# Hybrid encoder layer on one core: the wide output group's block sums formed by accumulating DRAM transfers, and one sum kept in DRAM

## The chip, the cores and the metric

One core of one Trainium2 chip. The metric is device time in microseconds (us); the median of three runs is given, with the lowest and highest. A profile shows one execution, with the time from its first to its last instruction (the span).

## What is computed

The layer is `x + mixed @ w_out`. x is 512 tokens by 2048, all float32. `mixed` has 2048 columns: 1024 from attention (8 heads, 2 key/value heads, QK norm, axial rope) and 1024 from a bidirectional gated linear recurrence (LRU), each normalised and gated by a SiLU of its own projection.

```
h = rms_norm(x, norm_w)
q, k, v, g_attn, xr, g_lru = split(h @ w_in)
attn_out = attention_group(q, k, v, ...)
lru_out = lru_group(xr, ...)
mixed = concat(rms_norm(attn_out) * silu(g_attn), rms_norm(lru_out) * silu(g_lru))
out = x + mixed @ w_out
```

The change touches only how parts of `w_out` are brought to the last half of the output columns.

## The kernel before

Every float32 operand is split into a high part (ScalarE's copy with rounding, "hi") and a low part (VectorE's subtraction, "lo"), and a product is three matmuls: hi by hi, hi by lo, lo by hi (`mm3`, L147 to L150; in the output, `product`, L845). Weights come as 256 rows by 512 columns (512 KB) through a ring of three buffers: `wraw` (L192, transfer L198, on SyncE's queue) and `wsplit` (L203: hi on ScalarE L209, lo on VectorE L210). The order on TensorE is written out by hand. On the other engines a scheduler orders the work by priority: `tc.high_priority(n)` moves work forward, `tc.issue_after(ins)` queues work behind an instruction on that engine. Each engine and each queue runs its list in order.

The stages: the LRU's input (two groups of 512 columns), K and V (`kv_proj`, L1008, woven with the second half of the LRU), Q in two groups (`both`, L1026, woven with K's norm, rope and transposes), attention woven with the gates' projections, then the output. In K and Q GpSimd raises mean squares to the power -1/2 (`rsqrt_mean`, L261 and L262): K's and Q's norms on VectorE (L518) wait for it.

The output has four groups of 512 columns. Groups 0 and 1 are made by `outputs` one after the other; groups 2 and 3 together by `outputs_wide` (L817), "the wide group". There the matrix is cut into 2 by 2 blocks and multiplied with Winograd's seven products (P1, P2, Q3 to Q7). `w_out` is walked in eight pairs of 128-row blocks, in the order 4 to 7, 0 to 3. Of a pair, row block k and column group j give four blocks of 128 by 512: call them B(k, j). The sums that the products need are

- T1 = B(0,0) + B(0,1)
- T2 = B(1,0) + T1
- T3 = B(0,0) + B(1,0)
- T4 = the sum of all four

Pass 1 (L856) takes P1, Q6 and Q5 over the eight pairs: 18 matmuls for each pair. It loads B(0,0) and B(0,1) in one transfer and B(1,0) in another (`raw_blocks`, L832), forms T1 in place of B(0,0) (VectorE, L861) and T2 in place of B(1,0) (L862), and `parts` splits all three (ScalarE L841, VectorE L842). Pass 2 (L909) takes Q3 and P2 of the plain blocks B(1,0) and B(1,1) (`plain`, L894), and Q7 and Q4 of T3 and T4 (`summed`, L899): 24 matmuls for each pair. It loads all four blocks again in two transfers of 512 KB, forms T3 and B(0,1) + B(1,1) in one add of 1024 elements (L903), T4 in a second add (L904), and splits plain and summed blocks apart. So a pair in pass 2 has a plain split and a summed split.

Three raw buffers of [4, 512] are used in turn, two in `aring` and one in `wring`; a buffer is free when its last split is done. The split parts have three buffers in turn too (`wkept`, L722). Between the passes, four adds (L871, L873) and copies (L869, L874) empty PSUM into the result tiles xs[0] ("xt") and xs[1] ("cb"). The residual x is added to them in pass 2 by `residual` (L876): four transfers of 512 KB (L880) into tiles "t4", of which there are two (`bufs=2`), each followed by one add on VectorE (L884): xt, cb, xt, cb. At the end the last products are added and the result leaves (L927, L930).

The TensorE rows of the trace carry the line of the matmul (L148 to L150, L752, L765, L851); "pj" and "mm" are the two kinds of PSUM tiles.

Of the kernel before, what the change touches and what calls it, by code (L numbers as in the profile page):

```python
# [10 lines left out]
F32 = mybir.dt.float32  # L11
F32R = mybir.dt.float32r
AF = mybir.ActivationFunctionType
ALU = mybir.AluOpType
AX = mybir.AxisListType

P = 128
SEQ = 512
DM = 2048
# [39 lines left out]
def hybrid_kernel(  # L59
# [20 lines left out]
    nc = tc.nc  # L80
# [30 lines left out]
    def nm(s):  # L111
        cnt[0] += 1
        return f"{s}_{cnt[0]}"
# [7 lines left out]
    def k2(dt=F32, shape=(P, SEQ)):  # L121
        pool, n, _ = work()
        return pools[pool].tile(list(shape), dt, tag="k2", bufs=n, name=nm("k2"))
# [11 lines left out]
    def pj():  # L135
        return ps.tile([P, SEQ], F32, tag="pj", name=nm("pj"))
# [7 lines left out]
    def f(ap):  # L144
        return ap.bitcast(F32)
# [43 lines left out]
        return vec[:, r : r + 1]  # L189


    def wraw(w, r0, c0, nk=1, queue=nc.sync):  # L192

        raw = wring.tile([P, 2, SEQ], F32, name=nm("wr"))
        src = w[r0 : r0 + 2 * P, c0 : c0 + SEQ].rearrange("(k p) e -> p k e", p=P)
        for k in range(nk):
            ks = slice(k * 2 // nk, (k + 1) * 2 // nk)
            queue.dma_start(raw[:, ks, :], src[:, ks, :])  # L198
            yield raw

    turn_of = [0]
# [131 lines left out]
    def weave(fill, chain):  # L333

        for n in chain:
            for _ in range(n):
                next(fill, None)
# [46 lines left out]
    def lru_half(half, acc):  # L384

        grs = []
        for n in range(4 * half, 4 * half + 4):
            gr = k2(shape=(P, 4, P))
            with tc.high_priority(AHEAD):
                nc.sync.dma_start(gr[:, 0:2, :], lru_wa[:, n].rearrange("d c e -> c d e"))  # L390
                nc.sync.dma_start(gr[:, 2:4, :], lru_wx[:, n].rearrange("d c e -> c d e"))
            grs.append(gr)
        xrs = evac_bc(acc)
        for b in range(0, 4, 2):
            bs = slice(b, b + 2)
            steps = ((6, 4, 8, 4), (10, 5, 8, 5))[half][bs]
            yield from lru_pair(4 * half + b, xrs[bs], grs[bs], steps, 99 if half and b else 0)
# [410 lines left out]
    def part(i, a):  # L808
# [5 lines left out]
            return [t[:, a + 1] for t in mixed[i][1]]  # L814
        return [t[a - 3] for t in sums_of[i]]

    def outputs_wide(c, built):  # L817


        xs = [  # L820
            pools["out"].tile([P, NT, SEQ], F32, tag=t, bufs=1, name=nm(t)) for t in ("xt", "cb")
        ]
        cs = [slice((c + j) * SEQ, (c + j + 1) * SEQ) for j in range(2)]
        rings = [aring, aring, wring]

        def raw_blocks(i, n, turn):

            raw = rings[turn % 3].tile([P, 4, SEQ], F32, name=nm("wr"))
            r0 = mixed[i][0]
            for k in range(2):  # L830
                w = slice(cs[0].start, cs[0].start + min(2, n - 2 * k) * SEQ)
                nc.sync.dma_start(  # L832
                    raw[:, 2 * k : min(n, 2 * k + 2)].rearrange("p j e -> p (j e)"),
                    w_out[r0 + k * P : r0 + (k + 1) * P, w],
                )
            return raw

        def parts(blocks, n):
            hi, lo = (t.rearrange("p n e -> p (n e)") for t in wkept(7))
            hi, lo = (t[:, : n * SEQ].rearrange("p (n e) -> p n e", e=SEQ) for t in (hi, lo))  # L840
            nc.scalar.copy(hi, blocks)  # L841
            nc.vector.tensor_sub(lo, blocks, f(hi))  # L842
            return hi, lo

        def product(k, dst, i, b, n):  # L845
            ah, al = part(i, k[0])
            bh, bl = (t[:, n] for t in b)
            for s in range(2):
                ts_ = slice(s * P, (s + 1) * P)
                for j, (lh, rh) in enumerate(((ah, bh), (ah, bl), (al, bh))):  # L850
                    nc.tensor.matmul(  # L851
                        dst[s], lh[:, ts_], rh, start=i == 0 and j == 0, stop=i == 7 and j == 2
                    )

        p1, q6, q5 = [pj(), pj()], [pj(), pj()], [mm(), mm()]
        for i in range(8):  # L856

            with tc.high_priority(SOON), tc.issue_after(built):
                raw = raw_blocks(i, 3, i)

                nc.vector.tensor_add(raw[:, 0], raw[:, 0], raw[:, 1])  # L861
                nc.vector.tensor_add(raw[:, 2], raw[:, 2], raw[:, 0])  # L862
                b = parts(raw[:, 0:3], 3)
            for k, dst, n in ((P1, p1, 1), (Q6, q6, 2), (Q5, q5, 0)):
                product(k, dst, i, b, n)
        with tc.high_priority(SOON):

            for s in range(2):
                nc.scalar.copy(xs[1][:, 2 + s], p1[s])  # L869
            for s in range(2):  # L870
                nc.vector.tensor_sub(xs[1][:, s], xs[1][:, 2 + s], q6[s])  # L871
            for s in range(2):
                nc.vector.tensor_sub(xs[0][:, 2 + s], q5[s], xs[1][:, s])  # L873
                nc.scalar.copy(xs[0][:, s], xs[0][:, 2 + s])  # L874

        def residual(m, j):  # L876

            with tc.high_priority(SOON):
                xr = pools["fin"].tile([P, 2, SEQ], F32, tag="t4", bufs=2, name=nm("t4"))
                nc.sync.dma_start(  # L880
                    xr, xf[2 * m * P : 2 * (m + 1) * P, cs[j]].rearrange("(t p) e -> p t e", p=P)
                )
            to = xs[j][:, 2 * m : 2 * m + 2]
            nc.vector.tensor_add(to, to, xr)  # L884

        q3, p2, q7, q4 = [mm(), mm()], [pj(), pj()], [pj(), pj()], [mm(), mm()]
        raws = {}

        def given(i):
            if i not in raws:  # L890
                raws[i] = raw_blocks(i, 4, 8 + i)
            return raws[i]

        def plain(i):  # L894
            with tc.high_priority(SOON):
                b = parts(given(i)[:, 2:4], 2)
            return lambda: product(Q3, q3, i, b, 0), lambda: product(P2, p2, i, b, 1)

        def summed(i):  # L899
            with tc.high_priority(SOON):  # L900
                raw = given(i)

                nc.vector.tensor_add(raw[:, 0:2], raw[:, 0:2], raw[:, 2:4])  # L903
                nc.vector.tensor_add(raw[:, 1], raw[:, 1], raw[:, 0])  # L904
                b = parts(raw[:, 0:2], 2)
            product(Q7, q7, i, b, 0)
            product(Q4, q4, i, b, 1)

        for i in range(6):  # L909
            for step in plain(i):  # L910
                step()
            summed(i)
            if 1 <= i < 5:
                residual((i - 1) // 2, (i - 1) % 2)

        summed(6)
        summed(7)
        for steps in zip(plain(6), plain(7)):
            for step in steps:
                step()  # L920

        with tc.high_priority(SOON):

            def add(t, j, acc, op=ALU.add, leave=True, cut=1):
                for m in range(cut):
                    e = slice(m * SEQ // cut, (m + 1) * SEQ // cut)
                    nc.vector.tensor_tensor(xs[j][:, t, e], xs[j][:, t, e], acc[:, e], op=op)  # L927
                    if leave:
                        to = slice(cs[j].start + e.start, cs[j].start + e.stop)
                        nc.sync.dma_start(of[tokens[t], to], xs[j][:, t, e])  # L930

            for s in range(2):
                add(s, 0, q7[s])
                add(s, 1, q7[s], ALU.subtract, False)
            for s in range(2):
                add(s, 1, q4[s])
            for s in range(2):
                add(2 + s, 0, q3[s])
            for s in range(2):
                add(2 + s, 1, p2[s], cut=1 + s)  # L940
# [5 lines left out]
    a1, a2, a3, a4, a5 = [], [], [], [], []  # L946
# [15 lines left out]
    with tc.high_priority():  # L962
        xs, ws = xload(0, 2), wraw(w_in, 0, C_XR, 2, nc.scalar)
        nc.scalar.dma_start(nw_st, norm_w.rearrange("(k p) -> k p", p=P))
        xc, raw = next(xs), next(ws)
# [9 lines left out]
    for step in proj_feat(C_XR, a1, first, given):  # L975
# [8 lines left out]
        c, e = step  # L984
# [17 lines left out]
    fill = proj_feat(C_XR + SEQ, a2)  # L1002
# [5 lines left out]
    def kv_proj():  # L1008
        yield from proj_tok(C_K, a3)
        kvs.extend(  # L1010
            evac_tok(
                a3, lambda: pools["rope"].tile([P, SEQ], F32, tag="kv", bufs=NT, name=nm("kv"))
            )
        )

    weave(kv_proj(), lru_half(1, a2))
    closed("lru")
    opened("rot", "left")
    opened("qkv", "right")
# [6 lines left out]
    def both():  # L1026
        yield from q_proj(C_Q, a4)
        yield from q_proj(C_Q + SEQ, a5)

    fill = both()  # L1030
    weave(fill, kv(kvs))
    drain(fill)

# [22 lines left out]
    fill = gates()  # L1056
# [11 lines left out]
    mixed = [[(NH + 2 * q) * P, None] for q in range(4)] + [[2 * q * P, None] for q in range(4)]  # L1068
# [30 lines left out]
    fill = proj_feat(C_GA + SEQ, acc)  # L1099
# [89 lines left out]
```

## Time and profile before

| what | value |
|---|---|
| median of 3 runs | 661.93 us (661.31 to 662.49) |
| the profiled execution | 660.99 us |
| its span | 659.2 us, mean granted TensorE clock 1.000 |
| TensorE, VectorE, ScalarE, GpSimd busy | 652.4, 500.8, 337.4, 58.9 us |
| moved by DMA | 77.32 MB, 117 GB/s in the mean |
| wide group on TensorE | 577.48 to 653.5 us |

PE is TensorE's matmuls, PEld its weight loads, DVE VectorE, ACT ScalarE, POOL GpSimd, SP SyncE; an engine's name with a q is its queue, or its sequencer. A row of the timeline gives start and duration in us, engine and line, what is written and read, partitions by elements, and in brackets how long the engine was idle before and what ended that. A row of a stage gives its limits, its length, the busy time of PE, PEld, DVE, ACT and POOL (with the number of instructions), the granted clock, the DMA engines' share and GB/s. A row of the chain gives start, duration, and the instructions merged in it. A row of waits gives who waited for whom, the total in us, how often, and the longest. A row of DMA issues ends in KB each and the median us from issue to landing.

### The profile page before, as it was taken

The numbers are of one execution on the slowest core, as the hardware profiler recorded it, in microseconds if no ns is written. First come the engines' busy times: TensorE is split into PE (matmuls) and PEld (weight loads), VectorE is DVE, ScalarE is ACT, GpSimd is POOL, SyncE is SP. The second block draws the span as 40 slices with busy tenths as digits, with TensorE's granted clock in tenths as the row PEclk, the third lists the DMA queues.
The fourth block names the chain that finished last, engine by engine and source line by source line (L and its number), as shares of the span: only waits on it lengthen the run. The fifth ranks groups of instructions, "written<-read, shape, count | busy, mean of one in ns | idle before, by whom it ended". The sixth has DMA issues, their size and how long they took to land.

```text
span 659.2 us, 8994 instructions
## 1 busy us (share of the span) xinstructions
PE 652.4 (99%) x3323; PEld 553.2 (84%) x3323; DVE 500.8 (76%) x822; ACT 337.4 (51%) x582; POOL 58.9 (9%) x79
## 2 busy tenths in 40 slices
PE   8999999999999999999999999999999999999996
PEld 6888888888888888888888888888889999888875
DVE  5889788978688854656955677439989998777995
ACT  3534898589766416444743455335437433233431
POOL 0000000000023303011222212110000000000000
PEclk9999999999999999999999999999999999999999
DMA  8852252323234312322112211232336356375643
GB/s 290 287 142 84 69 164 66 94 64 96 72 121 129 108 53 64 96 65 64 38 60 64 65 45 53 64 96 76 103 110 211 127 178 224 110 230 201 243 140 127
DMA packets 43963, 77.32 MB, mean 117 GB/s; under 512 B 2968, under 2 KB 13328, under 8 KB 43920
## 3 DMA queue, kind: packets, MB, share of 16 engines
q1 hardware_dynamic: 43600, 76.22, 37.5%
q10 hardware_dynamic: 320, 0.53, 0.3%
q8 instruction: 26, 0.43, 0.3%
q14 instruction: 17, 0.14, 0.1%
HBM read 72.54 MB, written 4.19 MB: 116 GB/s over the span
## 4 chain that ended last, share of the span: by engine, by line
PE 98%; DMA 1%; DVE 0%; ACTq 0%; DVEq 0%; issue 0%
PE pj L148 20%; PE pj L150 20%; PE pj L149 20%; PE pj L851 7%; PE pj L752 5%; PE mm L851 5%; PE mm L752 4%; PE mm L148 3%; PE mm L150 3%; PE mm L149 3%; PE mm L765 3%; PE mm L595 2%; PE mm L235 1%; PE pj L301 1%; PE mm L538 1%; DMA wr<-in_w_in_dram 1%
## 5 line engine op out<-in xcount | busy, mean ns | idle before, releaser
L148 PE MATMUL pj<-x,wh 128*128 128x512 f32 x376 | 149.1, 396 | 0.0
L150 PE MATMUL pj<-x,wl 128*128 128x512 f32 x376 | 147.0, 391 | 0.0
L149 PE MATMUL pj<-x,wh 128*128 128x512 f32 x376 | 146.5, 390 | 0.0
L210 DVE TENSOR_TENSOR wl<-wr,wh 128x512 fp32r<-128x512 f32 x144 | 100.8, 722 | 30.0 <-ACT wh L209 29.9
L209 ACT CAST wh<-wr 128x512 fp32r<-128x512 f32 x143 | 85.8, 618 | 73.4 <-PE pj L150 25.7
L150 PEld LDWEIGHTS pj<-x,wl 128*128 128x128 f32 x376 | 70.6, 188 | 15.3
L149 PEld LDWEIGHTS pj<-x,wh 128*128 128x128 f32 x376 | 70.7, 188 | 13.6 <-DVE x L238 0.2
L148 PEld LDWEIGHTS pj<-x,wh 128*128 128x128 f32 x376 | 70.6, 188 | 13.3
L148 PE MATMUL pj<-wh,x 128*128 128x512 f32 x192 | 74.9, 390 | 0.0
L150 PE MATMUL pj<-wh,x 128*128 128x512 f32 x192 | 74.7, 389 | 0.0
L149 PE MATMUL pj<-wl,x 128*128 128x512 f32 x192 | 74.7, 389 | 0.0
L841 ACT CAST wh<-wr 128x1024 fp32r<-128x1024 f32 (+1 forms) x24 | 28.7, 1198 | 52.0 <-PE mm L851 28.6
L597 ACT CAST b<-mm 128x512 fp32r<-128x512 f32 x32 | 18.8, 586 | 61.5 <-PE mm L595 61.5
L583 DVE TENSOR_REDUCE mx<-mm 128x1 f32<-128x512 f32 x32 | 22.0, 689 | 32.9 <-PE mm L150 32.3
L150 PEld LDWEIGHTS pj<-wh,x 128*128 128x128 f32 x192 | 36.0, 188 | 7.6
L148 PEld LDWEIGHTS pj<-wh,x 128*128 128x128 f32 x192 | 36.0, 188 | 7.5
L149 PEld LDWEIGHTS pj<-wl,x 128*128 128x128 f32 x192 | 36.0, 188 | 7.4
L588 POOL TENSOR_SCALAR k<-k,sm 128x512 f32<-128x512 f32 x32 | 24.2, 756 | 123.9 <-DVE sm L587 112.4
L842 DVE TENSOR_TENSOR wl<-wr,wh 128x1024 fp32r<-128x1024 f32 (+1 forms) x24 | 33.5, 1395 | 1.5 <-ACT wh L841 1.3
L598 DVE TENSOR_TENSOR b<-mm,b 128x512 fp32r<-128x512 f32 x32 | 22.1, 689 | 12.1 <-ACT b L597 12.1
L752 PE MATMUL pj<-wh,ml 128*128 128x256 f32 x96 | 27.2, 283 | 0.0
L752 PE MATMUL pj<-wl,mh 128*128 128x256 f32 x96 | 27.2, 283 | 0.0
(249 smaller groups left out, 1350.7 us busy)
## 6 DMA issues: line engine op xcount, KB each, us to landing
wr<-in_w_in_dram SPq DMA_DIRECT2D x71, 512.0 KB, 3.7
wr<-in_w_out_dram SPq DMA_DIRECT2D x40, 512.0 KB, 3.9
b<-in_x_dram SPq DMA_DIRECT2D x7, 512.0 KB, 8.9
out_dram<-xt SPq DMA_DIRECT2D x12, 256.0 KB, 3.2
xt<-in_x_dram SPq DMA_DIRECT2D x8, 256.0 KB, 5.0
wr<-in_w_out_dram SPq DMA_DIRECT2D x8, 256.0 KB, 4.3
t<-in_x_dram SPq DMA_DIRECT2D x4, 512.0 KB, 4.4
k<-in_lru_wa_dram SPq DMA_DIRECT2D x8, 128.0 KB, 3.6
```

Of the source, the lines that this page charges most:

```text
L148: nc.tensor.matmul(acc, lh, rh, start=start, stop=False)
L149: nc.tensor.matmul(acc, lh, rl, start=False, stop=False)
L150: nc.tensor.matmul(acc, ll, rh, start=False, stop=stop)
L209: copy(hi, raw[:, k, :])
L210: nc.vector.tensor_sub(lo, raw[:, k, :], f(hi))
L583: nc.vector.tensor_reduce(mx, sc, axis=AX.X, op=ALU.max, negate=True)
L588: nc.gpsimd.tensor_scalar(p, p, sm, 0.0, op0=ALU.mult, op1=ALU.add)
L598: nc.vector.tensor_sub(ptl[:, :, tt], p3, f(pth[:, :, tt]))
L752: nc.tensor.matmul(dst, lh[:, a, ts_], rh[:, b_, :], start=bank in fresh, stop=last and s == 1 and rh is bh and lh is al, skip_group_check ...
L841: nc.scalar.copy(hi, blocks)
L842: nc.vector.tensor_sub(lo, blocks, f(hi))
L851: nc.tensor.matmul(dst[s], lh[:, ts_], rh, start=i == 0 and j == 0, stop=i == 7 and j == 2)
```

## The change

T1 and T3 are formed in DRAM, long before they are used. During K and the first Q projection, after every two weight loads, SyncE copies B(0,0) of one pair into two DRAM tensors t1 and t3, queued behind the weight load issued last; then GpSimd issues two transfers which add B(0,1) to the one and B(1,0) to the other while moving (`accum_op`). Each waits for its copy. That makes 16 copies and 16 accumulating transfers of 256 KB.

In pass 1 T1 is loaded from t1, and the blocks B(0,1) and B(1,0) in transfers of their own; the add that formed T1 (L861) is gone. T2, formed as before, is also stored to a DRAM tensor t2. In pass 2 T3 and T2 are loaded from DRAM beside B(1,0) and B(1,1), four transfers of 256 KB in place of two of 512 KB; T4 is T2 + B(1,1), one add of 512 elements, and the add of 1024 (L903) is gone. The bytes that are loaded stay the same; eight stores of 256 KB come in.

```diff
+    loads_done = {}
     def wraw(w, r0, c0, nk=1, queue=nc.sync):
...
-            queue.dma_start(raw[:, ks, :], src[:, ks, :])
+            loads_done[queue] = queue.dma_start(raw[:, ks, :], src[:, ks, :]).ins
...
+    t1, t3, t2 = (
+        ctx.enter_context(tc.tile_pool(name=t, bufs=1, space=bass.MemoryType.DRAM)).tile(
+            [DM // (2 * P), P, SEQ + 16], F32, name=nm(t)
+        )[:, :, :SEQ]
+        for t in ("t1", "t3", "t2")
+    )
+    def sums_of_blocks(c):
+        pairs = w_out.rearrange("(m k p) e -> m k p e", k=2, p=P)
+        b12, b11 = (pairs[:, 0, :, (c + j) * SEQ : (c + j + 1) * SEQ] for j in range(2))
+        b22 = pairs[:, 1, :, c * SEQ : (c + 1) * SEQ]
+        for m in range(DM // (2 * P)):
+            with tc.issue_after(loads_done[nc.sync]):
+                for to in (t1, t3):
+                    nc.sync.dma_start(to[m], b12[m])
+            for to, other in ((t1, b11), (t3, b22)):
+                nc.gpsimd.dma_start(to[m], other[m], accum_op=ALU.add)
+            yield
...
-                raw = raw_blocks(i, 3, i)
-                nc.vector.tensor_add(raw[:, 0], raw[:, 0], raw[:, 1])
+                raw, m = raw_tile(i), mixed[i][0] // (2 * P)
+                for n, src in enumerate((t1[m], block(i, 0, 1), block(i, 1, 0))):
+                    nc.sync.dma_start(raw[:, n], src)
                 nc.vector.tensor_add(raw[:, 2], raw[:, 2], raw[:, 0])
                 b = parts(raw[:, 0:3], 3)
+                nc.sync.dma_start(t2[m], raw[:, 2])
...
-                raws[i] = raw_blocks(i, 4, 8 + i)
+                raw, m = raw_tile(8 + i), mixed[i][0] // (2 * P)
+                for n, src in enumerate((t3[m], t2[m], block(i, 1, 0), block(i, 1, 1))):
+                    nc.sync.dma_start(raw[:, n], src)
+                raws[i] = raw
...
-                nc.vector.tensor_add(raw[:, 0:2], raw[:, 0:2], raw[:, 2:4])
-                nc.vector.tensor_add(raw[:, 1], raw[:, 1], raw[:, 0])
+                nc.vector.tensor_add(raw[:, 1], raw[:, 1], raw[:, 3])
                 b = parts(raw[:, 0:2], 2)
...
+    wsums = sums_of_blocks(2)
+    def with_sums(fill, n):
+        for k, _ in enumerate(fill):
+            if k % n == n - 1:
+                next(wsums, None)
+            yield
-    weave(kv_proj(), lru_half(1, a2))
+    weave(with_sums(kv_proj(), 8), lru_half(1, a2))
...
-    fill = both()
+    fill = with_sums(both(), 8)
```

`block(i, k, j)` is B(k, j) of pair i in `w_out`, `raw_tile(turn)` one of the three raw buffers. A projection makes 32 steps over eight loads, so every eighth step is every second load: four pairs in K, four in the first Q.

More of the change, by code (lines that the diff above doesn't have):

```diff
@@ L824, in outputs_wide, with raw_tile, block @@
         rings = [aring, aring, wring]
[L826 to L836, printed above, removed]
+        def raw_tile(turn):
+            return rings[turn % 3].tile([P, 4, SEQ], F32, name=nm("wr"))
+        def block(i, k, j):
+            r0 = mixed[i][0] + k * P
+            return w_out[r0 : r0 + P, cs[j]]
         def parts(blocks, n):
```

## The prediction, made before the result was known

> **What bounds the kernel now.** I read the page first: its span, its first part and its chain.
>
> ```profile
> span 659.2 us, 8994 instructions
> PE 652.4 (99%) x3323; PEld 553.2 (84%) x3323; DVE 500.8 (76%) x822; ACT 337.4 (51%) x582; POOL 58.9 (9%) x79
> PE 98%; DMA 1%; DVE 0%; ACTq 0%; DVEq 0%; issue 0%
> ```
>
> TensorE is both the busy engine and the chain. A busy share can hide small waits, so next come busy time by stage, the chain in order of time in the stage that the change rewrites, and who waited there.
>
> ```profile
> 577.00:654.00 77.00, 77.00 (x339) 62.97 (x337) 62.22 (x66) 27.87 (x26) 0.00 (x0) 1.00 0.58 191
> ```
> ```profile
> 606.04 2.77 PE pj L851 x12
> 608.81 2.72 PE mm L851 x12
> ...
> 619.69 2.72 PE mm L851 x12
> 622.41 2.72 PE pj L851 x12
> 625.13 2.95 PE mm L851 x12
> 628.08 2.90 PE pj L851 x12
> ...
> 653.53 1.10 DVE cb L927 x2
> ```
> ```profile
> PEld mm L851 <- DVE wl L842: 0.4, 1, 0.4
> ```
>
> In the wide group TensorE is busy for 77.00 of 77 us at clock 1.00, and twelve products take 2.72 us, 0.227 each, wherever one looks. Two pieces are longer, 2.95 and 2.90: there alone TensorE waited for VectorE's split (the weight load of the first shows it, wl L842), (2.95 - 2.72) + (2.90 - 2.72) = 0.41 us. That is all that a lighter VectorE can give back here. VectorE's 62.22 busy us are off the path, and the 5.7 us from 653.53 to the end of the span are not touched. So the question is whether anything the change adds makes TensorE wait.
>
> **What it removes.** The built program of the changed kernel has TensorE's and ScalarE's instructions in the same order as before; VectorE loses 16 of 32 adds, SyncE gains 48 transfers, GpSimd 16.
>
> ```profile
> L903 DVE TENSOR_TENSOR wr<-wr x8: 1215/1222/1226, 599.3 to 638.9; 128x1024 f32<-128x1024 f32 x8
> L904 DVE TENSOR_TENSOR wr<-wr x8: 681/683/693, 600.5 to 640.2; 128x512 f32<-128x512 f32 x8
> L861 DVE TENSOR_TENSOR wr<-wr x5: 681/683/691, 576.9 to 594.1; 128x512 f32<-128x512 f32 x5
> ```
>
> Pass 1 loses eight adds of 0.68 (L861), pass 2 eight of 1.22 (L903); the other add of each pass stays. That is 8 x 0.68 + 8 x 1.22 = 15.2 us of VectorE, on the path only for the 0.41 above.
>
> **What moves.** VectorE's order changes in pass 2, and this is where I find the price. The residual's transfers (L880) use two buffers in turn: the third (x for xt's second half) can start only when the add of the first (L884) is done. Before, the third and fourth adds stand well behind:
>
> ```profile
> 602.91 0.80 SPq L832 DMA_DIRECT2D wr<-in_w_out_dram  x2
> ```
> ```profile
> 608.11 1.23 DVE L903 TENSOR_TENSOR wr<-wr 128x1024 f32<-128x1024 f32 x1 [2.35 <-DMA wr<-in_w_out_dram]
> 609.25 1.22 DVE L842 TENSOR_TENSOR wl<-wr,wh 128x1024 fp32r<-128x1024 f32 x1
> 610.38 1.28 DVE L871 TENSOR_TENSOR cb<-cb,pj 128x512 f32<-128x512 f32 x2
> 610.49 0.80 SPq L832 DMA_DIRECT2D wr<-in_w_out_dram  x2
> 611.58 1.28 DVE L873 TENSOR_TENSOR xt<-mm,cb 128x512 f32<-128x512 f32 x2
> ...
> 614.51 1.22 DVE L884 TENSOR_TENSOR xt<-xt,t 128x1024 f32<-128x1024 f32 x1
> 615.76 0.38 SPq L880 DMA_DIRECT2D t<-in_x_dram  x1
> ...
> 621.93 1.22 DVE L884 TENSOR_TENSOR xt<-xt,t 128x1024 f32<-128x1024 f32 x1
> ...
> 625.38 1.22 DVE L842 TENSOR_TENSOR wl<-wr,wh 128x1024 fp32r<-128x1024 f32 x1
> ```
> ```profile
> SPq L880 <- DVE xt L884: 4.4, 1, 4.4
> t<-in_x_dram SPq DMA_DIRECT2D x4, 512.0 KB, 4.4
> ```
>
> The first residual add starts at 614.51, its buffer's next transfer is issued at 615.76 (SyncE waited 4.4 us for exactly this), and the add that uses it stands at 621.93, seven VectorE instructions later. In the changed program's VectorE order the stretch reads: T4 add of pair 2, summed split of pair 0, the four adds of L871/L873, the second residual add (cb), plain split of pair 1, **T4 add of pair 3, first residual add (xt), summed split of pair 1, third residual add (xt), plain split of pair 2**. One split stands between the add that frees the buffer and the add that waits for its refill; behind that wait is a split which TensorE needs.
>
> Step by step, with start-to-start times from the fence: 1.14 us for 1024 elements (609.25 - 608.11), 0.60 for 512 (two from 610.38 to 611.58), 5.2 us from the first issue of a pair's 1 MB to the add (602.91 to 608.11).
> - Pair 2's four transfers start when pass 1's last split has freed their buffer, as before (602.9); I take 603.0. T4 add of pair 2 at 608.2, split of pair 0 at 608.8, free at 609.95.
> - Four adds from 609.95, 4 x 0.60: 612.35; second residual add to 613.5; plain split of pair 1 to 614.65.
> - Pair 3's transfers start at 610.05 into the buffer of pair 0 (before 610.49) and land 5.2 later: T4 add of pair 3 at 615.25 (before, the add stood later, at 616.78, and did not wait). First residual add 615.85 to 617.0, summed split of pair 1 to 618.15.
> - The third residual transfer starts at 617.1 (0.1 after the add, as 615.76 after 614.51 + 1.14) and lands 4.4 later, 621.5. Its add runs to 622.65, the plain split of pair 2 is done at 623.85.
> - TensorE: the piece at 619.69 ends with the first product of pair 2, from 621.05; its second matmul, at 621.28, reads the split's low part. Before, the split of pair 3 ended at 625.38 + 1.22 = 626.60 and the matmul it held came at 625.13 + 7 x 0.227 + 0.23 = 626.95, 0.35 behind. So here: 623.85 + 0.35 = 624.2, **2.9 us late**.
>
> Behind this everything has 2.9 us more: the fourth residual add to 624.95, summed split of pair 2 to 626.1, needed at 624.0 + 2.9 = 626.9; the later pairs are spaced as before. The 0.41 of the two long pieces disappears in the new wait.
>
> Sum: 2.9 - 0.4 = +2.5 us. Its own profiled execution took 660.99 us (1.8 outside the span), so 663.5; the median of three is 0.94 above that: **664.4**.
>
> **What else is added, at nothing.** Copies and accumulations during K and Q: 32 of 256 KB, four per two weight loads.
>
> ```profile
> 185.69 0.37 SPq L198 DMA_DIRECT2D wr<-in_w_in_dram  x1
> ```
> ```profile
> 192.46 0.27 POOL L261 TENSOR_SCALAR rr<-rr 128x2 f32<-128x2 f32 x1 [1.78 <-ACT sh L513]
> 193.87 0.42 DVE L518 TENSOR_TENSOR kv<-kv,rr 128x256 f32<-128x256 f32 x1 [0.19 <-POOL rr L262]
> 197.03 1.88 DVE L210 TENSOR_TENSOR wl<-wr,wh 128x512 fp32r<-128x512 f32 x3
> 211.60 0.68 ACT L501 ACTIVATE ev<-pj,rstd 128x512 f32<-128x512 f32 x1
> ```
> ```profile
> xt<-in_x_dram SPq DMA_DIRECT2D x8, 256.0 KB, 5.0
> ```
>
> SyncE issues the copies behind a weight load, 0.4 us each, in time it otherwise waits. GpSimd's queue is in order: the last two accumulations stand ahead of K's second rsqrt (192.46) and wait for copies issued behind the load of 185.69. No copy between two DRAM tensors is in the trace; by a 256 KB load they land at 186.5 + 5.0 = 191.5. GpSimd's own time to issue one is not in the trace either; the nearest are SyncE's 0.37 and its own 0.27, so 0.3 to 1.5 each, and rsqrt is 0 to 2 us late. VectorE waits with it at 193.87, and the split behind, at 197.03, is late by as much. It feeds Q0's last load: the last bank was evacuated at 211.60, one load is 24 x 0.227 = 5.4 us of products, so it is read from about 206. Some 8 us of cover: cost nothing.
>
> The Trainium skill, "DMA: Bandwidth & Descriptors", section "Specifications", gives about 1 us to the first byte of a DMA issued by GpSimd against 0.6 from SyncE; by an estimate from it rsqrt would be 2 us late, inside the same cover, and the sum stays; no run here shows it yet.
>
> T2's stores: pair 0's T2 is stored in pass 1 and loaded a pass later, eight pairs on (8 x 18 x 0.227 = 33 us), so the two landings do not meet. The eight stores (256 KB) stand between pass 1's loads in SyncE's queue, each behind a VectorE add. The tightest of pass 1's splits, for pair 3, and the piece that reads it:
>
> ```profile
> 585.18 1.75 DVE L842 TENSOR_TENSOR wl<-wr,wh 128x1536 fp32r<-128x1536 f32 x1
> 589.72 2.72 PE pj L851 x12
> ```
>
> It ends at 586.9, 2.8 us early. In the new order it stands ahead of pair 4's add, for which it waited, and comes sooner; stepped in the same way, the later ones end within 1 us of before. So nothing; with the cover gone, up to 3 us.
>
> The same page of the Trainium skill, section "Rules for kernel authors", says that a DMA which reads what an earlier one wrote must wait for its completion, so T2 pays two landings; were store and load close, pass 2's first loads would be late by one more landing, which no run here shows yet.
>
> **The rivals.**
> - *A, the refill is in time, not slower.* If a pair's four transfers land faster than the two before (VectorE is lighter, the DMA engines are 0.58 busy), the whole row of waits moves forward. For no loss the plain split of pair 2 must end by 621.28 - 0.35 = 620.9, the third residual add start by 618.6, its transfer by 614.2, so that pair 3 has landed by 612.3, 2.9 us sooner than I step. Against it: 5.2 us to land, and buffers that TensorE's pace frees. With 1 MB in 4 us the first residual add ends near 615.7 (pass 1's last products hold the adds of L871/L873) and +1.2 is left. At best the 0.41 is won: 661.5.
> - *B, pass 1 goes late too.* SyncE holds the next loads behind each store; if a store's add slips, splits lose their 3 us of cover and TensorE waits there as well, on top: 2.5 + 1 to 3 us, 665.5 to 667.5. For it: six more waits in SyncE's order; against: the step above.
> - *C, GpSimd's wait in K and Q.* If an accumulation holds GpSimd until rsqrt is over 8 us late (copies landing after some 13 us instead of 5), TensorE waits for the rest; at 12 us 4 more, 668. Transfers of this size never took that long here.
>
> **How the numbers follow.** Forecast, one stalled split at +1.4 to +4.5 us: 0.60. A: 0.27. B: 0.10. C: 0.03. The bounds of the forecast's own unknowns (landing of 1 MB 5.0 to 6 us, of 512 KB 3.7 to 5.5) give 663.3 to 666.4. The range reaches into A's best, 661.4, and over B, 667.8. 0.2% is 1.3 us, about what a measurement of this kernel can tell from no change. Slower by more: forecast, B, C, a little of A: 0.73. Within: 0.25. Faster: 0.02.
>
> **What would show it.** Right: in pass 2 a VectorE wait of about 3 us of the third residual add (xt) for `t<-in_x_dram`, a TensorE or weight-load wait of about 3 us for the split next to it near 621, none before 618, and the rest of the chain shifted alike. GpSimd's 16 issues inside 94 to 194 us without a wait of TensorE. Wrong: no gap near 621 (A), gaps from 585 to 606 (B), gaps from 195 to 215 (C).

## The result and the profile after

The changed kernel takes **668.81 us** (median of 4 runs, 667.24 to 669.12) against 661.94 (661.31 to 662.49) for the kernel before: 1.0097 times as long, 95% interval 1.0084 to 1.0110. It is slower, as forecast, but by 6.9 us where 2.5 was forecast, and lies above the range, which ended at 667.8. The profiled execution took 668.51 us.

The page of the changed kernel (span; busy time of each engine; the chain by engine):

```profile
span 666.7 us, 9091 instructions
...
PE 656.2 (98%) x3323; PEld 554.9 (83%) x3323; DVE 488.1 (73%) x806; ACT 337.5 (51%) x582; POOL 73.0 (11%) x95
...
PE 57%; DMA 5%; DVE 3%; SPq 2%; issue 1%; ACT 1%; DVEq 0%; ACTq 0%
```

VectorE is lighter by 12.7 us (500.8 to 488.1), as intended, and nothing came of it. The chain, before TensorE from end to end, now runs through DMA, VectorE and SyncE's queue. The busy time of the wide group and TensorE's waits tell where:

```profile
577.00:654.00 77.00, 72.99 (x311) 58.74 (x310) 45.04 (x45) 27.32 (x26) 0.00 (x0) 0.98 0.64 198
```
```profile
PE pj L871 <- DVE wl L862: 3.1, 2, 2.2
...
PE mm L871 <- DVE wl L862: 0.9, 1, 0.9
PE pj L148 <- ACT ev L504: 0.2, 1, 0.2
```

TensorE idles 4 of 77 us and its clock falls from 1.00 to 0.98. Three waits are for a split (L862), one for ScalarE's emptying of a PSUM bank in Q (L504). The longest, in the timeline of TensorE (start, duration, the idle time in brackets):

```profile
606.81 0.39 PE L871 MATMUL mm<-wh,ev 128*128 128x512 f32 x1
607.04 0.39 PE L871 MATMUL pj<-wh,mh 128*128 128x512 f32 x1
609.63 0.73 PE L871 MATMUL pj<-wl,mh 128*128 128x512 f32 x1 [2.20 <-DVE wl L862]
610.15 0.63 PE L871 MATMUL pj<-wh,ml 128*128 128x512 f32 x1
610.58 0.63 PE L871 MATMUL pj<-wh,mh 128*128 128x512 f32 x1
...
612.71 0.60 PE L871 MATMUL pj<-wh,ml 128*128 128x512 f32 x1
613.14 0.40 PE L871 MATMUL pj<-wh,mh 128*128 128x512 f32 x1
613.38 0.40 PE L871 MATMUL pj<-wl,mh 128*128 128x512 f32 x1
```

Starts that stood 0.23 apart are 2.59 apart at 607.04, and then 0.43 apart from 610.15 to 613.14: seven steps of 0.427 instead of 0.227. One wait is paid twice: 2.36 us at the wait, 0.29 in the first step after it, and 1.4 in the seven slow steps. The granted clock in these slow steps (a row of a stage, for TensorE alone) is 0.50:

```profile
609.75:613.10 3.35, 3.35 (x8) 0.50 0.71 207
```

The two other waits, at 620.86 and 624.83, cost 1.2 each and leave the clock alone. From the start of its first matmul to the start of its last the wide group takes 83.0 us (578.24 to 661.24) where it took 76.5 (577.31 to 653.79): that is +6.5 of the span's +7.5. The rest, 0.93, lies before it: 0.56 at the wait in Q and 0.37 in the first 46 us, where TensorE waits for the first loads and every execution differs (its first real product began at 6.13 before, at 5.89 to 6.97 in the runs below). Hence the table below has a column for the wide group alone.

What the late split stood behind is in VectorE's order:

```profile
587.27 0.69 DVE L883 TENSOR_TENSOR wr<-wr 128x512 f32<-128x512 f32 x1 [1.43 <-DMA wr<-in_w_out_dram]
589.43 0.69 DVE L883 TENSOR_TENSOR wr<-wr 128x512 f32<-128x512 f32 x1 [1.46 <-DMA wr<-in_w_out_dram]
...
596.55 0.69 DVE L883 TENSOR_TENSOR wr<-wr 128x512 f32<-128x512 f32 x1 [4.76 <-DMA wr<-in_w_out_dram]
...
607.21 0.69 DVE L928 TENSOR_TENSOR wr<-wr 128x512 f32<-128x512 f32 x1 [6.03 <-DMA wr<-in_w_out_dram]
607.82 1.75 DVE L862 TENSOR_TENSOR wl<-wr,wh 128x1536 fp32r<-128x1536 f32 x1
...
615.49 0.69 DVE L928 TENSOR_TENSOR wr<-wr 128x512 f32<-128x512 f32 x1 [3.66 <-DMA wr<-in_w_out_dram]
```

The split of pass 1's last pair (607.82, three blocks) stands behind pass 2's first T4 add (L928), and that waited 6.03 us for a transfer. Three adds ahead of it in pass 1 waited too, the last of them 4.76 us. SyncE's queue shows why the one at 596.55 did:

```profile
585.87 0.33 SPq L881 DMA_DIRECT2D wr<-t  x1
587.99 2.48 SPq L885 DMA_DIRECT2D t<-wr  x2
590.51 1.36 SPq L881 DMA_DIRECT2D wr<-in_w_out_dram  x2
```

T1 of pair 6 is requested at 585.87; then SyncE holds at two stores of T2 (L885) until the adds of 587.27 and 589.43 are done, and the pair's two other blocks go out from 590.51, 4.6 us after the first.

### The profile page after: what moved, and what is told of

The parts are those of the page before. It is cut to its first block, busy times and chain, and to the rows that moved or that the text cites. A ratio compares the mean times of both kernels' runs of the same rounds, so it can differ in the third digit from the quotient of the medians.

```text
span 666.7 us, 9091 instructions
## 1 busy us (share of the span) xinstructions
PE 656.2 (98%) x3323; PEld 554.9 (83%) x3323; DVE 488.1 (73%) x806; ACT 337.5 (51%) x582; POOL 73.0 (11%) x95
## 2 busy tenths in 40 slices
DMA packets 53180, 87.81 MB, mean 132 GB/s; under 512 B 3992, under 2 KB 14352, under 8 KB 53136
## 4 chain that ended last, share of the span: by engine, by line
PE 57%; DMA 5%; DVE 3%; SPq 2%; issue 1%; ACT 1%; DVEq 0%; ACTq 0%
PE pj L148 11%; PE pj L150 11%; PE pj L149 11%; DMA wr<-in_w_out_dram 5%; PE pj L755 4%; PE mm L755 3%; PE mm L871 3%; PE pj L871 3%; PE mm L148 2%; PE mm L150 2%; PE mm L149 2%; PE mm L598 2%; PE mm L768 2%; DVE wl L862 1%; SPq L881 1%
## 5 line engine op out<-in xcount | busy, mean ns | idle before, releaser
L150 PEld LDWEIGHTS pj<-x,wl 128*128 128x128 f32 x376 | 70.6, 188 | 15.2
L861 ACT CAST wh<-wr 128x1024 fp32r<-128x1024 f32 (+1 forms) x24 | 28.5, 1196 | 54.6 <-PE mm L871 15.1
L862 DVE TENSOR_TENSOR wl<-wr,wh 128x1024 fp32r<-128x1024 f32 (+1 forms) x24 | 33.4, 1398 | 6.3 <-ACT wh L861 6.3
L838 POOL DMA_DIRECT2D t<-in_w_out_dram x16 | 13.3, 834 | 132.0 <-DMA t<-in_w_out_dram 132.0
L871 PE MATMUL pj<-wl,mh 128*128 128x512 f32 x60 | 24.5, 408 | 3.1 <-DVE wl L862 3.1
```

The lines of the kernel that those rows point to most:

```text
L150: nc.tensor.matmul(acc, ll, rh, start=False, stop=stop)
L871: nc.tensor.matmul(dst[s], lh[:, ts_], rh, start=i == 0 and j == 0, stop=i == 7 and j == 2)
```

## The experiments

After this reading there were two theories for the wide group. **L**: the loads themselves are slower, since a pair comes in four transfers of one block (256 KB) where two double blocks came. **S**: SyncE is held at T2's stores and issues the next loads late. K and Q are a third, smaller item. The results, all beside runs of the kernel before on the same chip (medians 661.2 to 661.9); the last column is worked out as above from each profile, so from one execution:

| run | median us | ratio, 95% interval | wide group on TensorE, us |
|---|---|---|---|
| before | 661.9 | | 76.5 |
| changed kernel | 668.8 | 1.0097 (1.0084 to 1.0110) | 83.0 |
| e1, T2 not stored | 666.4 | 1.0067 (1.0052 to 1.0082) | 81.3 |
| e2, T2 stored by GpSimd | 665.4 | 1.0056 (1.0043 to 1.0069) | 81.5 |
| e3, before + sums in K and Q | 662.7 | 1.0018 (1.0009 to 1.0026) | 78.2 |
| e4, before, single blocks | 666.8 | 1.0078 (1.0066 to 1.0090) | 80.8 |
| e5, before, small extra transfers | 661.8 | 1.0003 (0.9993 to 1.0013) | 76.1 |
| e6, before, 2 KB rows | 664.5 | 1.0044 (1.0029 to 1.0060) | 77.8 |
| e7, changed, long rows in pass 2 | 662.9 | 1.0017 (1.0005 to 1.0029) | 78.0 |
| e8, e7 with all sums in K | 662.7 | 1.0011 (1.0001 to 1.0022) | 78.2 |
| e9, e8 with long rows in pass 1 too | 661.3 | 1.0001 (0.9992 to 1.0011) | 76.0 |
| e10, before, half transfers | 671.3 | 1.0146 (1.0131 to 1.0162) | 87.4 |
| e11, e9 with stores by SyncE | 661.5 | 1.0004 (0.9995 to 1.0013) | 76.1 |

### e1 and e2: T2's stores

e1 leaves out the store and forms T2 again in pass 2, from B(0,1) in place of t2 and a second add:

```diff
-                nc.sync.dma_start(t2[m], raw[:, 2])
...
-                for n, src in enumerate((t3[m], t2[m], block(i, 1, 0), block(i, 1, 1))):
+                for n, src in enumerate((t3[m], block(i, 0, 1), block(i, 1, 0), block(i, 1, 1))):
...
+                nc.vector.tensor_add(raw[:, 1], raw[:, 1], raw[:, 0])
```

e2 only moves it to GpSimd's queue: `nc.gpsimd.dma_start(t2[m], raw[:, 2])`.

> The changed kernel, without T2 in DRAM: no store in pass 1, and in pass 2 B(0,1) is loaded in T2's place and T4 = T3 + B(0,1) + B(1,1), one more add of 512 on VectorE for each pair. The bytes loaded and the number of loads stay. Theory S (the T2 stores stand in SyncE's queue ahead of the next pair's loads, each behind a VectorE add that waits for a load, so loads cannot run ahead): the waits of TensorE in the wide group go, and with them most of the 6.9 us; 661.5 to 663.5 us, what is left being the K and Q part. Theory L (single-block transfers of 256 KB land later than the double blocks before, whatever the queue): waits of TensorE stay, 665 us or more. Theory V (VectorE's order, the next pair's add ahead of the split, is enough alone): 665 or more too, with the wait at the split of pass 1's last pair.

> The changed kernel with T2's eight stores issued from GpSimd's queue, which is empty in this stage; bytes and loads as changed. Theory S: SyncE's loads are free again, no wait of TensorE at the split of pass 1's last pair, 661.5 to 664. If the traffic of the stores (2.1 MB more in the wide group) delays the loads: about as the changed kernel, 667 to 669. Theory L: 665 or more.

Both stay far above before: 2.4 and 3.4 us less than the changed kernel, 4.8 and 3.8 us more than the kernel before beside them. The long stall moves into pass 2's start (behind the matmuls of 613.15 and 613.87, 2.1 us idle each), where TensorE waits for PSUM that VectorE empties late, and both again run some 3 us at spacing 0.427 behind it. The first matmul after it, in e1:

```profile
615.64 0.65 PE L871 MATMUL pj<-wh,mh 128*128 128x512 f32 x1 [2.10 <-DVE cb L892]
```

So S is a part, at most half; with no store at all most of the loss is left. e1 is the less clean of the two, since it has eight adds more on VectorE.

### e3 and e4: one part alone in the kernel before

e3 adds the copies and accumulations of K and Q to the kernel before, and nothing uses them. e4 leaves the kernel before as it is, VectorE's adds too, and only loads each block by itself:

```diff
-            for k in range(2):
-                w = slice(cs[0].start, cs[0].start + min(2, n - 2 * k) * SEQ)
-                nc.sync.dma_start(
-                    raw[:, 2 * k : min(n, 2 * k + 2)].rearrange("p j e -> p (j e)"),
-                    w_out[r0 + k * P : r0 + (k + 1) * P, w],
-                )
+            for n_ in range(n):
+                k, j = n_ // 2, n_ % 2
+                nc.sync.dma_start(raw[:, n_], w_out[r0 + k * P : r0 + (k + 1) * P, cs[j]])
```

> The kernel before with the K and Q part alone: copies and accumulating transfers are made, and the wide group does not use them. Reading of the changed trace: GpSimd's second rsqrt of K is 2.5 us late behind the last two accumulations, and ScalarE's evacuation of Q's first bank with it, so TensorE waits about 0.5 us near 210: 662.2 to 662.8. If the first projection's 0.37 us later start also comes from the change: 662.8 to 663.2. If the copies cost nothing: 661.9.

> The kernel before with one transfer of 256 KB for each block in the wide group (three a pair in pass 1, four in pass 2), no sums in DRAM. Theory S: SyncE has spare time and nothing waits in its queue, within 0.2% of before, 661 to 663. Theory L: each pair's blocks land about 1 us later than in double transfers, VectorE's adds wait longer, TensorE waits in the wide group: 664 or more.

e4 alone costs 5.2 us, with the same bytes and the same order on every engine but SyncE. **L holds.** e3 costs 1.1 us, and of that 0.63 us lies between 112 and 223 us in its profile, where the changed kernel lost 0.64. Its wide group, whose instructions are those of before, was 1.7 us longer, with one wait of 1.4 at 629: so near its edge is the kernel before, and so far can a figure of the last column lie off with the wide group's instructions unchanged.

### e5, e6 and e10: what of the split costs

Single blocks differ in two things: more transfers, and rows of 2 KB in DRAM instead of 4 KB. e5 issues a further transfer of 1 KB behind each 512 KB load (VectorE's order differs in four places); e6 keeps two transfers of 512 KB but cuts them as two row blocks of one column group (VectorE's order differs in five places, near 565); e10 halves each by partitions.

```diff
+                    with tc.issue_after(load):
+                        nc.sync.dma_start(spare[small[0] % 8][:16], w_out[r0 : r0 + 16, :16])
```
```diff
+            for j in range(2):
+                nk = min(2, n - 2 * j)
+                nc.sync.dma_start(
+                    raw[:, j : j + 2 * nk - 1 : 2],
+                    w_out[r0 : r0 + nk * P, cs[j]].rearrange("(k p) e -> p k e", p=P),
+                )
```
```diff
+                for h in range(nj):
+                    ps = slice(h * P // nj, (h + 1) * P // nj)
+                    rs = slice(r0 + k * P + ps.start, r0 + k * P + ps.stop)
+                    nc.sync.dma_start(
+                        raw[ps, 2 * k : 2 * k + nj].rearrange("p j e -> p (j e)"), w_out[rs, w]
+                    )
```

> The kernel before, with a further transfer of 1 KB issued behind each of the wide group's 512 KB loads: as many issues on SyncE as with one transfer per block (four for a pair of pass 2), but the rows stay 4 KB long. Theory N (the number of transfers costs: 0.4 us of SyncE each, so that the second load of a pair starts 0.8 later instead of 0.4): 664.5 to 667, with waits of TensorE between the passes as in the run with single blocks. Theory R (the length of the rows costs: a transfer of 2 KB rows keeps the DMA engines busy longer for the same bytes): 661.3 to 662.3, no change.

> The kernel before, with the same number of transfers of the same sizes in the wide group, but each 512 KB transfer takes two row blocks of one column group (256 rows of 2 KB) instead of one row block of two column groups (128 rows of 4 KB). Theory N: 661.3 to 662.3, no change. Theory R: 665 to 667, landing of a 512 KB transfer 4.5 us or more against 3.9 before, and a DMA share of about 0.8 from 577 to 602 against 0.73.

> The kernel before, with each 512 KB load of the wide group cut into two transfers of 64 rows of 4 KB: as many transfers of 256 KB as in the run with single blocks, but long rows. VectorE's order in the wide group changes too, since the scheduler prices the halves otherwise. If the number of real transfers costs (each of 256 KB keeps the engines longer than half of one of 512 KB): 664 to 667, DMA share up as with single blocks (its queue's packets took 38.3% of the span against 37.5). If only the length of the rows does: 661.3 to 663.

Neither e5 nor e6 gives e4's time. Their traces say why, at one place that all share: the loads of pass 2's third pair, and the first add that reads them. In the kernel before these rows stand in the prediction (issued 602.91 to 603.71, add at 608.11). SyncE, then VectorE, of e4, of e6 and of e5 (in e5 the real loads are L833, the small ones L840):

```profile
605.47 1.76 SPq L832 DMA_DIRECT2D wr<-in_w_out_dram  x4
```
```profile
612.05 1.23 DVE L900 TENSOR_TENSOR wr<-wr 128x1024 f32<-128x1024 f32 x1 [3.73 <-DMA wr<-in_w_out_dram]
```
```profile
606.39 0.88 SPq L832 DMA_DIRECT2D wr<-in_w_out_dram  x2
```
```profile
612.08 1.22 DVE L903 TENSOR_TENSOR wr<-wr 128x1024 f32<-128x1024 f32 x1 [2.84 <-DMA wr<-in_w_out_dram]
```
```profile
602.51 0.33 SPq L833 DMA_DIRECT2D wr<-in_w_out_dram  x1
602.88 0.43 SPq L840 DMA_DIRECT2D spare<-in_w_out_dram  x1
603.36 0.42 SPq L833 DMA_DIRECT2D wr<-in_w_out_dram  x1
```
```profile
608.23 1.23 DVE L908 TENSOR_TENSOR wr<-wr 128x1024 f32<-128x1024 f32 x1 [1.45 <-DMA wr<-in_w_out_dram]
```

Each add waits for its transfer, so the add marks the landing. From the end of the last issue it is 4.40 us in before (608.11 - 603.71), 4.45 in e5, 4.81 in e6, 4.82 in e4: rows of 2 KB cost 0.4 here. Before that, each further issue of SyncE takes 0.47: two end 0.80 after the first began, four 1.76. From first issue to add that makes **5.2 us before, 5.7 in e5 and in e6, 6.6 in e4**. Some 0.5 us more is just what the kernel before covers: e5 shows no change, e6 is 2.5 us slower (1.3 of it in the wide group of its profile; there T1 too has to wait for both transfers, which may be the difference). It does not cover 1.4. The same pair takes 6.75 in e1 (605.68 to 612.43) and 6.58 in e2 (607.32 to 613.90). In the changed kernel it takes 5.9 (609.60 to 615.49), issued late and behind the long stall; there pass 2's first pair is the slow one, 8.3 (598.94 to 607.21), with a store of T2 issued between its loads. A raw buffer's next load starts when its last one is used up, so lateness adds from round to round: measured from each wide group's start, e4's loads begin 0.2 us later than before's for pass 2's first pair (595.26 and 594.19), 1.7 for the third (605.47 and 602.91), 3.0 for the fourth (614.43 and 610.49).

e10 does not tell its two cases apart. It took 671.3, but TensorE waits nowhere before 642.6; then the splits of the last pairs stand in an order that the scheduler made for the halves, in which ScalarE waits for a split buffer that TensorE still holds:

```profile
643.06 1.99 ACT L844 CAST wh<-wr 128x1024 fp32r<-128x1024 f32 x2 [5.46 <-PE mm L854]
650.89 1.99 ACT L844 CAST wh<-wr 128x1024 fp32r<-128x1024 f32 x2 [5.84 <-PE mm L854]
```

Two stalls of 2.1 us of TensorE, each with one of 0.9 close behind, and half the clock from 646.4 for 3.4 us and from 653.2 for 6.8 us make the loss. That is an order, not a load. What real transfers of 256 KB with long rows cost is left open.

### e7, e8, e9 and e11: the changed kernel with the old pattern of loads

e7 keeps T3 and T2 side by side in one DRAM tensor, so that pass 2 loads a pair in two transfers of 512 KB with 4 KB rows; the stores go by GpSimd. e8 also issues all sums in K. e9 keeps T1 beside a copy of B(0,1), so that pass 1 loads as before too. e11 is e9 with the stores on SyncE, as in the changed kernel. Cut out are e7's loads of pass 2, e8's weave in K, and e9's loads of pass 1:

```diff
-                for n, src in enumerate((t3[m], t2[m], block(i, 1, 0), block(i, 1, 1))):
-                    nc.sync.dma_start(raw[:, n], src)
+                r0 = mixed[i][0] + P
+                for n, src in enumerate((t32[m], w_out[r0 : r0 + P, cs[0].start : cs[1].stop])):
+                    nc.sync.dma_start(
+                        raw[:, 2 * n : 2 * n + 2].rearrange("p j e -> p (j e)"), src
+                    )
...
-    weave(with_sums(kv_proj(), 8), lru_half(1, a2))
+    weave(with_sums(kv_proj(), 3), lru_half(1, a2))
...
-                for n, src in enumerate((t1[m], block(i, 0, 1), block(i, 1, 0))):
-                    nc.sync.dma_start(raw[:, n], src)
+                nc.sync.dma_start(raw[:, 0:2].rearrange("p j e -> p (j e)"), t1[m])
+                nc.sync.dma_start(raw[:, 2], block(i, 1, 0))
```

> The changed kernel with T3 and T2 side by side in one DRAM tensor, so that pass 2 again loads a pair in two transfers of 512 KB with 4 KB rows, and with T2's stores issued by GpSimd; pass 1 keeps its three single transfers. If the split of pass 2's loads and SyncE's waits at the stores are the cause (both N and R say so): 662 to 663.5, no wait of TensorE above 0.5 us between 606 and 627, and the 0.5 us of K and Q left. If the sums themselves or T2's way through DRAM cost (theory M, memory traffic of 10 MB more): 665 or more, as with the changed kernel.

> As the repaired kernel, with all copies and accumulations issued in K after every third step, none in Q: GpSimd has issued the last one well before K's rsqrt. If the late rsqrt is what holds TensorE at 210: 0.4 to 0.6 us less than the repaired kernel, 661.4 to 663, and no wait at 210. If the denser traffic in K holds K's own weight loads: as long as the repaired kernel or longer, with waits of TensorE between 150 and 195.

> As the repaired kernel with its sums in K, and T1 kept beside B(0,1) in one DRAM tensor (the copy takes both blocks), so that pass 1 too loads a pair as before: 512 KB in 4 KB rows and 256 KB. VectorE keeps its 15.2 us less, T2 still goes through DRAM by GpSimd. If the pattern of the loads is the whole cause in the wide group: 661.3 to 662.2, the wide group on TensorE within 0.5 us of before's 76.5 from its first matmul to its last (the two repaired kernels with short rows in pass 1 were 1.6 and 1.7 over that). If T2's stores and loads, or what VectorE's new order does, cost by themselves: 662.5 to 664, with waits of TensorE of over 1 us between 606 and 627.

> As the run with long rows in both passes, with T2's stores issued by SyncE again, as in the changed kernel: the stores wait for their adds in the queue that also issues the next pair's loads. If SyncE's wait at the stores costs even with loads as fast as before: 2 to 3 us over the run with long rows (the changed kernel lost 3.4 by it, 668.8 against 665.4 with GpSimd's stores). If it cost only because the loads were already late: within 0.7 us of the run with long rows.

e7 takes 6.0 us off the changed kernel. Against e2 it differs in the pattern of pass 2's loads (and in the layout of the tensor that they read), with the same order of instructions on TensorE, VectorE and ScalarE, and that is worth 2.5 us (665.4 to 662.9). Two waits of TensorE are left there, 0.7 and 0.5 us before the matmuls of 617.52 and 621.02; the expectation had none above 0.5. e9 stands at the kernel before; its interval and e8's overlap, so what pass 1's rows are worth by themselves is not shown by the medians. e9's page and its wide group:

```profile
span 659.1 us, 9039 instructions
...
PE 651.9 (99%) x3323; PEld 553.5 (84%) x3323; DVE 487.8 (74%) x806; ACT 336.9 (51%) x582; POOL 76.7 (12%) x103
...
PE 98%; DMA 1%; DVE 0%; ACTq 0%; DVEq 0%; issue 0%
```
```profile
601.27 0.32 SPq L917 DMA_DIRECT2D wr<-t  x1
601.63 0.43 SPq L917 DMA_DIRECT2D wr<-in_w_out_dram  x1
```
```profile
606.52 0.69 DVE L932 TENSOR_TENSOR wr<-wr 128x512 f32<-128x512 f32 x1 [1.91 <-DMA wr<-in_w_out_dram]
```

The same pair is there 5.25 us after the first issue, 4.46 after the last, as before, and no wait of TensorE is left in the wide group. e9 moves more bytes than the changed kernel (89.91 MB against 87.81), keeps the sums in DRAM, T2's way through it and VectorE's 13 us less, and loses nothing: **the pattern of the loads was the cause in the wide group**. The two long pieces are gone too, and the wide group is 0.4 us shorter than before, in e9 and in e11; in the medians that cannot be seen (0.9992 to 1.0011). e5, with all of VectorE's adds, is 0.4 us shorter as well, so it is not shown that the lighter VectorE wins it. No version beat the kernel before.

e11 settles S. SyncE waits at the stores there as well, and VectorE's adds wait up to 4.2 us for their loads, but nothing of it reaches TensorE, and it costs 0.2 us, within the intervals. SyncE's waits at the stores from 577 to 640, in the changed kernel and in e11:

```profile
SPq L885 <- DVE wr L883: 8.9, 5, 3.9
```
```profile
SPq L886 <- DVE wr L884: 3.8, 4, 2.3
```

In the changed kernel the stores cost 3.4 us (668.8 to 665.4), so their price hangs on the loads. By the rows above, each late load there made the add late, the add the store, the store the next load; that chain is read from one trace. e11 also answers theory V of e1's expectation: its TensorE, VectorE and ScalarE run the changed kernel's instructions in the same order, pass 1's last split behind pass 2's first T4 add too, so that order alone costs nothing that shows.

e8 against e7 gives no gain from moving the sums, 662.7 to 662.9, where 0.4 to 0.6 was expected if the late rsqrt held TensorE; e7's profile has no wait in Q although its instructions there are those of the changed kernel.

## Why the prediction was wrong, step by step

- **What bounds the kernel, the 0.41 us, VectorE off the path: right.** e9 wins that 0.4 in the wide group and nothing else from 13 us less VectorE. The 15.2 us were too many: VectorE's busy time fell by 12.7 in the changed kernel. The durations that I added overlap those of their neighbours; 0.60 and 1.14 from start to start would have given 13.9.
- **The forecast step, the third residual add behind the refill of the first one's buffer: failed.** SyncE issued the third residual transfer right after the second residual add, and the third add did not wait. SyncE, then VectorE:

```profile
621.00 4.33 SPq L902 DMA_DIRECT2D t<-in_x_dram  x2
```
```profile
619.75 1.23 DVE L906 TENSOR_TENSOR cb<-cb,t 128x1024 f32<-128x1024 f32 x1
...
625.97 1.22 DVE L906 TENSOR_TENSOR xt<-xt,t 128x1024 f32<-128x1024 f32 x1
...
628.97 1.23 DVE L906 TENSOR_TENSOR cb<-cb,t 128x1024 f32<-128x1024 f32 x1 [0.64 <-DMA t<-in_x_dram]
```

  I took the two buffers to alternate in the order of the source; here the buffer freed first by the new VectorE order, that of the second add, got the third transfer. TensorE did wait near 621 and 625, 0.9 us each, but for splits behind a late T4 add. The place agreed by accident.
- **"5.2 us from the first issue of a pair's 1 MB to the add", used for four transfers: this is the step that failed and cost most.** By e4 and e2 four single blocks take 6.6 (the first pair of the changed kernel 8.3), and each round of three buffers adds the difference again. I quoted the row that held the price, 0.80 us for two issues, and did not double it. The Trainium skill, "DMA: Bandwidth & Descriptors", section "Bandwidth", has the rule to batch transfers to 1 MiB or more; e4 against before (6.6 against 5.2 us for the same 1 MB) agrees with its direction.
- **"The later ones end within 1 us of before" in pass 1: failed.** The add at 596.55 waited 4.76 us. Rival B named this mechanism, SyncE holding the next loads behind a store, and gave it 1 to 3 us and a tenth of the chance; it took 3.4, together with the slower loads. TensorE's stall came at 607, though, not from 585 to 606: pass 1's last split stood behind pass 2's first add.
- **K and Q at nothing: the wrong consumer.** GpSimd's rows of the changed kernel, with the rsqrt behind the last two accumulations:

```profile
192.36 0.88 POOL L838 DMA_DIRECT2D t<-in_w_out_dram  x1 [1.31 <-DMA t<-in_w_out_dram]
194.05 0.82 POOL L838 DMA_DIRECT2D t<-in_w_out_dram  x1 [0.81 <-DMA t<-in_w_out_dram]
194.94 0.19 POOL L264 TENSOR_SCALAR rr<-rr 128x2 f32<-128x2 f32 x1
...
198.42 2.98 POOL L264 TENSOR_SCALAR rr<-rr 128x2 f32<-128x2 f32 x1 [1.15 <-ACT sh L516]
```

  The rsqrt is 2.5 us late (194.94 against 192.46); 0.37 of it is the later start of this execution, so about 2.1, the upper end of my 0 to 2. I had followed it to a split with 8 us of cover. But an add on VectorE stands behind the same norms, ScalarE waits for that add, and ScalarE's emptying of Q0's first PSUM bank stands behind that wait. It began at 209.56 where it had been 207.47, and TensorE needed the bank. The emptying, in the changed kernel and before:

```profile
209.56 0.68 ACT L504 ACTIVATE ev<-pj,rstd 128x512 f32<-128x512 f32 x1
```
```profile
207.47 0.68 ACT L501 ACTIVATE ev<-pj,rstd 128x512 f32<-128x512 f32 x1
```

  That cost about 0.6 us in the profiles of the changed kernel and of e3, and nothing in those of e1, e2 and e7, whose instructions there are the same and whose rsqrt is as late. What differs is a later rsqrt of GpSimd: its first instruction took 2.98 us in the changed kernel (198.42) and 3.05 in e3, but 0.36, 0.20 and 0.33 in e1, e2 and e7, and only in the first two did VectorE wait for it, 0.9 us (before, too, 0.87). Why it takes so differently long the traces do not show. Rival C, 8 us late, did not come.
- **The clock was in no sum.** 1.4 of the 6.5 us are matmuls at half speed behind a stall.

The 6.5 us of the wide group by its rows: 4.05 for the stall at 607 with its slow matmuls, 1.25 and 1.23 for the two later ones with the steps behind them, 0.2 each at 598.6 and 618.0, where single matmuls follow each other up to 0.1 us late, less the 0.4 that was won: 6.5.

## What to carry to other kernels

Where a row of buffers is refilled just in time, the price of a load is the time from its first issue to the last landing: count SyncE's time for each further issue (0.47 us here), look up what rows it reads, and add the difference again for each round of the ring, before counting what the consumer saves. A wait put into the queue that issues loads cost 0.2 us here while the loads had cover (e11), and 3.4 where they were late already. For a moved or added wait, follow the order of every engine behind it, not the one consumer that comes to mind.

## What the runs showed of the hardware

- **TensorE idle times of 2.1 to 2.2 us were followed by half the clock.** Behind one such wait matmuls start 0.427 us apart for about 3 us (changed kernel, e1, e2); in e10, where a wait of 0.9 stands close behind it, for 2.6 us the first time and 5.1 the second. Waits of 0.9 to 1.5 us (changed kernel, e3, e4) left the spacing at 0.23. The Trainium skill, "TensorE: Matmul & The Clock Gate", Part 1, gives 426.7 ns for this shape in the cold state, which agrees, and about 3.4 us of idle window before it, counted by a free-running window; here 2.1 us of idle time was enough. The stretches of one granted clock agree with such a window: in the changed kernel the clock falls at 609.73 and rises at 613.14, and its stretches last 604.16, 3.41 and 51.20 us, whole multiples of 3.41. Cut into windows of 3.41 us in this way, the four traces show 2.1 to 2.9 us idle in the window ahead of each fall within the wide group; up to 1.4 us in a window (e3, e4), and 1.6 at e10's end, changed nothing. Between 1.6 and 2.1 nothing was measured.
- Accumulating transfers took GpSimd 0.83 us each to issue (16, in the changed kernel) and landed 6.0 us after it; denser in K, 8.1 to 8.3 (e8, e9).
- The time before the first loads are there moves an execution by up to 1 us and more (e6 was 1.5 us later than before after 46 us, with the same instructions up to there), so a single profile's span is no measure of a change of 1 us.
